# Attention kernel: the second layer's modulation accumulated in a PSUM bank of its own, PV and value transposes on the other bank, GpSimd's low weight parts in two halves

## The chip, the cores and the metric

The kernel is one program on one core of a Trainium2 chip. A core has TensorE (PE in the profile), VectorE (DVE), ScalarE (ACT), GpSimd (POOL) and SyncE (SP), which here only issues DMAs. The metric is the device time of one execution in microseconds (us), the median of several runs. Less is better.

## The reference, cut to what matters

A network of two layers works on 1024 latent tokens and 256 context tokens of width 1024. Layer 0 is grouped-query attention, layer 1 a convolution module. Each layer is wrapped in a modulation: from a condition vector `c` one linear map gives a shift, a scale and a gate.

```python
for i in range(2):
    shift, scale, gate = split(silu(c) @ ada_w[i] + ada_b[i])      # 1024 -> 3 x 1024
    h = rmsnorm(x, norm_g[i]) * (1 + scale) + shift
    if i == 0:   # 16 query heads, 4 key/value heads of 128, rotary positions
        q, k, v, z = split(h @ w_in);  kc, vc = the same columns for the context
        p = softmax([sink, q @ kc.T, q @ k.T where |i - j| <= 128])
        y = ((p @ [vc, v]) * silu(z)) @ w_out
    else:        # pointwise GLU, depthwise convolution of width 31, layer norm, gate
        y = conformer(h)
    x = x + gate * y
out = rmsnorm(x, final_g)
```

Everything is in float32. The kernel computes each large product from a high and a low part of both operands (three of the four partial products), so each weight chunk is split: the high part is a rounded copy, the low part is what the copy lost.

## The kernel before

**Stages.** First come layer 0's shift and scale, the turned and normalised tokens (tiles `hh` and `hl`, high and low), and the projections k, q, v of head group 0. Then the attention stage walks through 128 steps, one for each of 16 heads and 8 blocks of 128 queries. Between its own products TensorE computes there the projections of later heads, 12 matmuls a step (`fill`). Then follow attention's output projection, layer 1's input projection with the convolution, and the output projection.

**A step of attention.** `scores` (line 967) forms the scores of the next block in a PSUM tile `pss`; VectorE adds the mask and takes the maximum (the custom operation into `p_page`), ScalarE takes exponentials, VectorE a reciprocal (`sc`), GpSimd scales the probabilities. `transposes` (line 1001) turns the current block's probabilities on TensorE; ScalarE and VectorE evacuate them as `pthi` and `ptlo`. Once four blocks are there, `pv` (line 1022) multiplies them with the values into a PSUM tile `pso`, and VectorE evacuates it with the gate path into `oz_half`.

**Change of the key group.** After heads 3, 7 and 11 the projections k and v of the next group run whole. `vt_split` (line 550) turns a piece of v into `pso`, and ScalarE and VectorE evacuate it as `vh` and `vl`. The order on TensorE is: context piece, first half, `pv` of the old head's second half, scores of the new head, second half.

**The modulation that is left over.** `ada_rest` (line 582) is a generator that the steps advance once or twice each. It computes layer 0's gate and all of layer 1's modulation on VectorE: 16 chunks of 256 columns, 8 row blocks each. SP loads a block of 128x256 raw weights into one of two buffers (`dww_raw`, `wsum_raw`). VectorE multiplies it by the condition and adds it to the accumulator `acc_a`, 256 columns of the tile `mask_page` in SBUF. In a chunk's first block two small operations add the bias on a diagonal. After the eighth block TensorE sums over the partitions by a product with a column of ones into a tile `pso`. A gate chunk goes back into the first row of `acc_a` and from there to DRAM (`gd`); another goes into `mod1`.

**Banks.** `ps_o()` (line 128) gives one of two PSUM banks (512 columns each), in turn unless a number is asked for. `pv`, `vt_split` and `ada_rest` took turns. In the projections of group 0 the turns of x tiles ask for bank 0 or 1 by the parity of their index.

**Weight chunks.** `WStream.split` (line 221) makes a chunk's high part on ScalarE (`whi_page`) and its low part (`wlo_page`, 128x1024) on VectorE or, for all of the attention's chunks but the first four, on GpSimd. Layer 1's chunks take another branch of it, which isn't changed. `low_parts` splits the output weights on ScalarE (`lhi_half`) and GpSimd (`low_page`) and stores their low parts to DRAM (`wolA`, `wolC`).

**What sets the order.** TensorE's instructions stay in the order of the program. For the other engines and the DMA queues a planner lays out the order beforehand: it simulates the program with costs of its own and takes, of what is ready, what stands earliest or has its priority raised. On the chip every queue runs in that order. Accesses to one PSUM bank by two engines are kept apart by waits.

## Time and profile before

| what | value |
|---|---|
| runs | 1755.21, 1755.38, 1758.65 us; median 1755.38 |
| profiled execution | span of 1752.9 us; its own run time isn't listed beside the three, whose median is 2.5 us above the span |
| granted TensorE clock | 0.996 on the mean |
| TensorE busy | 1720.7 us, 98% of the span |
| VectorE, ScalarE, GpSimd busy | 1148.3, 889.4, 895.4 us |
| accumulations of `ada_rest` | first at 67.8 us, last at 824.6 us |

The span goes from the first to the last instruction. An engine's busy time is the union of its instructions' spans. All of this kernel's instructions are recorded under one line, a helper's, so the profile is read by the names of the tiles: `pss<-kh_page,qh_page` is a product of keys and queries into a tile `pss`.

### The profile page before, as it was taken

Reading aid. Unit: us, or ns where it says so; the run is one execution under the profiler, and the core shown is the slowest. Engines: PE = TensorE matmul, PEld = TensorE weight load, DVE = VectorE, ACT = ScalarE, POOL = GpSimd, SP = SyncE. Lnnn points to the kernel's source line nnn. Section 1 sums busy time; section 2 is a strip of 40 time slices with the busy share of each in tenths; the row PEclk is TensorE's granted clock in tenths of the full one; section 3 lists DMA queues with packets and bytes.
Section 4 is the critical chain, followed back from the end, with each engine's and each line's share of the span. In section 5 each row is a group of like instructions: output and inputs, shape, how many; then the busy total and the mean of one; then the engine's idle time right before and its main releaser. Section 6 shows DMA issues by size and latency. Waiting matters only on the chain.

```text
span 1752.9 us, 23877 instructions
## 1 busy us (share of the span) xinstructions
PE 1720.7 (98%) x8420; PEld 1424.8 (81%) x8420; DVE 1148.3 (66%) x2079; ACT 889.4 (51%) x1548; POOL 895.4 (51%) x705
## 2 busy tenths in 40 slices
PE   7999999999999999999999999999999999999997
PEld 4788888888888888888888888888888888788886
DVE  6755564556546563656315189999999999867823
ACT  7555553445345444545334355554665564466731
POOL 0245654566636565653101267998898888130300
PEclk9999999999999999999999999999999999999999
DMA  9334443444334542436777733011121202377971
GB/s 313 107 82 139 136 133 85 145 147 145 100 105 143 152 142 87 136 119 203 279 250 239 241 90 105 13 54 31 43 79 36 91 30 79 120 254 243 325 264 48
DMA packets 195324, 242.45 MB, mean 138 GB/s; under 512 B 11798, under 2 KB 126790, under 8 KB 195204
## 3 DMA queue, kind: packets, MB, share of 16 engines
q1 hardware_dynamic: 188516, 230.10, 40.3%
q10 hardware_dynamic: 6688, 10.83, 2.6%
q8 instruction: 66, 1.08, 0.3%
q14 instruction: 54, 0.44, 0.1%
HBM read 188.70 MB, written 41.69 MB: 131 GB/s over the span
## 4 chain that ended last, share of the span: by engine, by line
PE 86%; DMA 5%; DVE 3%; POOL 2%; ACT 2%; issue 2%; SPq 1%; ACTq 0%; POOLq 0%; DVEq 0%
PE psg L89 44%; PE pss L89 22%; PE pso L89 19%; DMA araw_page<-in_ada_w_dram 1%; POOL rope_half L89 1%; DMA low_page<-in_conv_w_out_dram 1%; DMA rope_half<-rope_half 1%; SPq L89 1%; DMA low_page<-in_attn_w_out_dram 1%; DMA wolC<-low_page 1%; DVE mask_page L89 1%; ACT p_page L89 0%; POOL wlo_page L89 0%; POOL low_page L89 0%; DMA wraw_page<-in_attn_w_in_dram 0%
## 5 line engine op out<-in xcount | busy, mean ns | idle before, releaser
L89 POOL TENSOR_TENSOR odd_half<-odd_half,prod_half 128x513 f32<-128x513 f32 (+2 forms) x252 | 312.8, 1250 | 24.2 <-ACT prod_half L89 11.0
L89 PE MATMUL psg<-hh_page,whi_page 128*128 128x512 f32 x600 | 237.6, 396 | 0.0
L89 PE MATMUL psg<-hh_page,wlo_page 128*128 128x512 f32 x600 | 236.9, 395 | 0.0
L89 PE MATMUL psg<-hl_page,whi_page 128*128 128x512 f32 x600 | 236.8, 395 | 0.0
L89 POOL TENSOR_TENSOR wlo_page<-wraw_page,whi_page 128x1024 fp32r<-128x1024 f32 x70 | 173.1, 2475 | 104.1 <-ACT whi_page L89 83.2
L89 ACT ACTIVATE prod_half<-ubuf,dww 128x513 f32<-128x513 f32 (+2 forms) x252 | 165.1, 674 | 107.3 <-POOL odd_half L89 105.1
L89 POOL TENSOR_SCALAR p_page<-p_page,sc 128x640 f32<-128x640 f32 (+1 forms) x128 | 100.8, 787 | 224.4 <-DVE sc L89 208.7
L89 PE MATMUL psg<-h2h_page,whi_page 128*128 128x512 f32 x464 | 183.9, 396 | 0.0
L89 PE MATMUL psg<-h2h_page,wlo_page 128*128 128x512 f32 x464 | 183.0, 394 | 0.0
L89 PE MATMUL psg<-h2l_page,whi_page 128*128 128x512 f32 x464 | 182.4, 393 | 0.0
L89 DVE SCALAR_TENSOR_TENSOR pss<-ubuf,dww,pss 128x512 f32<-128x512 f32 (+3 forms) x270 | 172.3, 670 | 0.1
L89 DVE SCALAR_TENSOR_TENSOR pss<-ubuf,wsum,pss 128x512 f32<-128x512 f32 (+3 forms) x270 | 171.7, 670 | 0.2
L89 DVE TENSOR_TENSOR ptlo<-pss,pthi 128x640 fp32r<-128x640 f32 (+1 forms) x144 | 103.3, 717 | 64.0 <-ACT pthi L89 62.8
L89 ACT ACTIVATE p_page<-p_page,sc 128x641 f32<-128x641 f32 (+1 forms) x128 | 102.7, 802 | 74.1 <-DVE sc L89 69.7
L89 ACT ACTIVATE pthi<-pss 128x640 fp32r<-128x640 f32 (+1 forms) x144 | 88.6, 615 | 91.7 <-PE pss L89 86.3
L89 PEld LDWEIGHTS psg<-hh_page,wlo_page 128*128 128x128 f32 x600 | 112.9, 188 | 26.3
L89 PEld LDWEIGHTS psg<-hh_page,whi_page 128*128 128x128 f32 x600 | 113.0, 188 | 20.8 <-DVE kvc_page L89 0.2
L89 PEld LDWEIGHTS psg<-hl_page,whi_page 128*128 128x128 f32 x600 | 112.9, 188 | 20.7
L89 ACT ACTIVATE whi_page<-wraw_page 128x1024 fp32r<-128x1024 f32 x88 | 92.6, 1053 | 69.0 <-PE psg L89 25.5
L89 PE MATMUL pso<-h2l_page,whi_page 128*128 128x512 f32 x304 | 119.9, 394 | 0.0
L89 PE MATMUL pso<-h2h_page,whi_page 128*128 128x512 f32 x304 | 119.8, 394 | 0.0
L89 PE MATMUL pso<-h2h_page,wlo_page 128*128 128x512 f32 x304 | 119.6, 394 | 0.0
(244 smaller groups left out, 4105.2 us busy)
## 6 DMA issues: line engine op xcount, KB each, us to landing
wraw_page<-in_conv_w_in_dram SPq DMA_DIRECT2D x48, 512.0 KB
wraw_page<-in_attn_w_in_dram SPq DMA_DIRECT2D x40, 512.0 KB
wol_page<-wolA SPq DMA_DIRECT2D x32, 512.0 KB
wo_page<-in_attn_w_out_dram SPq DMA_DIRECT2D x32, 512.0 KB
wo_page<-in_conv_w_out_dram SPq DMA_DIRECT2D x32, 512.0 KB
wol_page<-wolC SPq DMA_DIRECT2D x32, 512.0 KB
rope_half<-rope_half ACTq DMA_DIRECT2D x80, 128.0 KB
araw_page<-in_ada_w_dram SPq DMA_DIRECT2D x32, 256.0 KB
```

Of the source, the lines that this page charges most:

```text
L89: r = f(*a, **k)
```

## The change

There are three edits. The accumulator of `ada_rest` becomes columns 0 to 255 of PSUM bank 1, which it holds for its whole life; TensorE's sum goes into columns 256 to 511 of the same bank, and before that sum ScalarE copies the accumulator to its old place in `mask_page`, with raised priority. `vt_split` and `pv` always ask for bank 0. And where GpSimd makes a chunk's low part in the unraised branch of `split`, it does so in two operations of half the chunk each.

```diff
@@ WStream.split
-                split_lo(self.lo_eng(i), l, r, h)
+                if self.lo_eng(i) is G:
+                    for a in range(0, KT, KT // 2):
+                        split_lo(G, *(t[:, a:a + KT // 2] for t in (l, r, h)))
+                else:
+                    split_lo(self.lo_eng(i), l, r, h)
@@ vt_split
-        tp = ps_o()
+        tp = ps_o(0)
@@ ada_rest
         load(0)
+        bank = ps_o(1)
+        acc, o = bank[:, 0:256], bank[:, 256:512]
         for i, (l, c0, kt) in enumerate(todo):
...
             if kt == 0:
-                after(V.tensor_scalar(out=acc_a, in0=raw, scalar1=cs[:, kt:kt + 1], scalar2=None, op0=ALU.mult))
+                after(V.tensor_scalar(out=acc, in0=raw, scalar1=cs[:, kt:kt + 1], scalar2=None, op0=ALU.mult))
                 for b in range(2):
...
-                    stt(acc_a[:, bs], ident, abt[:, col:col + 1], acc_a[:, bs], ALU.mult, ALU.add)
+                    stt(acc[:, bs], ident, abt[:, col:col + 1], acc[:, bs], ALU.mult, ALU.add)
             else:
-                after(stt(acc_a, raw, cs[:, kt:kt + 1], acc_a, ALU.mult, ALU.add))
+                after(stt(acc, raw, cs[:, kt:kt + 1], acc, ALU.mult, ALU.add))
             yield
             if kt < KT - 1:
                 continue
+            with tc.high_priority():
+                act(acc_a, acc, AF.Copy)
             yield
-            o = ps_o()
             if c0 >= 2048:
-                PE.matmul(o[0:1, 0:256], ones[:, 0:1], acc_a, start=True, stop=True)
-                V.tensor_copy(acc_a[0:1], o[0:1, 0:256])
+                PE.matmul(o[0:1], ones[:, 0:1], acc_a, start=True, stop=True)
+                V.tensor_copy(acc_a[0:1], o[0:1])
                 SY.dma_start(out=gd[l][:, c0 - 2048:c0 - 1792], in_=acc_a[0:1])
             else:
                 for b in range(2):
                     PE.matmul(o[:, b:b + 1], acc_a[:, b * P:b * P + P], ones[:, 0:1], start=True, stop=True)
                 V.tensor_copy(mod1[:, c0 // P:c0 // P + 2], o[:, 0:2])
@@ pv
-        o = ps_o()
+        o = ps_o(0)
```

## The prediction

> **What bounds the kernel now.** I read the busy shares first, then busy time by stage, then TensorE's own waits inside the stage that the change touches. From the page's first part and from the busy time of each engine in five stretches (columns: stretch, length, then busy us and instruction count of PE, PEld, DVE, ACT, POOL; granted clock; DMA share; GB/s):

> ```profile
> span 1752.9 us, 23877 instructions
> PE 1720.7 (98%) x8420; PEld 1424.8 (81%) x8420; DVE 1148.3 (66%) x2079; ACT 889.4 (51%) x1548; POOL 895.4 (51%) x705
> ...
> 0.00:97.00 97.00, 83.66 (x402) 57.59 (x403) 62.57 (x114) 60.42 (x92) 13.58 (x17) 0.96 0.60 190
> 97.00:850.00 753.00, 745.04 (x4107) 642.27 (x4106) 424.05 (x832) 368.79 (x776) 412.08 (x340) 1.00 0.44 136
> 850.00:1050.00 200.00, 200.00 (x914) 163.27 (x913) 75.31 (x154) 74.08 (x115) 43.91 (x40) 1.00 0.62 208
> 1050.00:1500.00 450.00, 448.51 (x1937) 363.97 (x1936) 430.46 (x682) 256.71 (x360) 383.24 (x281) 1.00 0.19 57
> 1500.00:1753.00 253.00, 243.53 (x1067) 197.69 (x1065) 155.95 (x300) 129.43 (x206) 42.58 (x28) 0.99 0.62 215
> ```

> TensorE is the bound everywhere. The attention stage, where almost all of the change takes effect, runs from about 97 to 850 us; TensorE is busy for 745.04 of its 753 us. So 8 us is all that a perfect change of that stage could win, 0.45% of the time. The clock is at 1.00 there and the change adds no matrix work, so what counts is only which of those idle times go and which come. VectorE and GpSimd are 56% and 55% busy in that stage: their busy time alone buys nothing. TensorE's waits in it (columns: who waited for whom; us in total, times, longest):

> ```profile
> PE pss L89 <- DVE ptlo L89: 3.6, 2, 3.2
> PE pss L89 <- DVE sc L89: 1.3, 3, 0.9
> PE pss L89 <- POOL hl_page L89: 1.2, 1, 1.2
> PE psg L89 <- DVE rope_half L89: 1.0, 1, 1.0
> PE pss L89 <- POOL p_page L89: 0.5, 1, 0.5
> ```

> These are 7.6 of the 8 us, in eight waits. No wait on the tile pso, the two banks that the change rearranges, is among them.

> **Step 1: the accumulator moves to PSUM.** The 112 multiply-adds now read two tensors from SBUF (the raw weights and the accumulator in mask_page). The convolution stage does the same operation with its accumulator in PSUM, and is the nearest row for the price after. From the groups with shapes kept apart (count | busy us, mean ns):

> ```profile
> L89 DVE SCALAR_TENSOR_TENSOR mask_page<-wsum_raw,cs,mask_page 128x256 f32<-128x256 f32 x64 | 51.3, 801 | 0.1
> L89 DVE SCALAR_TENSOR_TENSOR mask_page<-dww_raw,cs,mask_page 128x256 f32<-128x256 f32 x48 | 38.4, 800 | 3.0 <-DMA dww_raw<-in_ada_w_dram 2.9
> L89 DVE SCALAR_TENSOR_TENSOR pss<-ubuf,dww,pss 128x264 f32<-128x264 f32 x30 | 14.0, 490 | 0.0
> L89 DVE SCALAR_TENSOR_TENSOR pss<-ubuf,dww,pss 128x248 f32<-128x248 f32 x30 | 13.3, 468 | 0.0
> ```

> Halfway between 490 and 468 is 479 ns for 256 columns. The operation gets 0.32 us shorter on the mean, 112 x 0.32 = 36 us of VectorE (estimate). Why it is 801 now shows in the stretch around 546 us (start us, us, engine, operation, [idle before it and what ended that]):

> ```profile
> 544.88 1.28 POOL L89 TENSOR_TENSOR low_page<-low_page,lhi_half 128x512 f32<-128x512 f32 x1
> 545.18 1.26 DVE L89 SCALAR_TENSOR_TENSOR mask_page<-wsum_raw,cs,mask_page 128x256 f32<-128x256 f32 x1
> 546.36 0.87 DVE L89 CUSTOM_DVE_ANT_0 p_page<-pss,mask_page,nsink 128x640 f32<-128x640 f32 x1
> ...
> 547.30 0.44 PE L89 MATMUL pss<-kh_page,qh_page 128*128 128x384 f32 x1 [0.19 <-DVE sc L89]
> ```

> The multiply-add starts while GpSimd runs a two-input subtraction, ends 0.28 us after it (546.16), and takes 1.26 us; the softmax's mask-and-maximum waits behind it on VectorE, and TensorE waits for that. All three waits on "DVE sc" have such a stretched operation just ahead of that maximum. With 0.48 us in place of 1.26, 0.78 us come back, more than the 0.19 lost here; I take the whole 1.3 us. The 48 other small operations on the accumulator are not counted; shorter ones could only help the same three places. Each raw buffer is free for SP's next load up to 0.78 us earlier; the number of DMAs is unchanged.

> VectorE also stops waiting where an accumulation could not begin before a gate row had left mask_page:

> ```profile
> DVE mask_page L89 <- DMA gd<-mask_page: 5.8, 4, 2.0
> ```

> None of TensorE's eight waits lies behind those four, so I count nothing for 5.8 us of VectorE.

> **Step 2: 16 copies on ScalarE, and the low parts in halves.** The rows for both prices:

> ```profile
> L89 ACT ACTIVATE pthi<-pss 128x256 fp32r<-128x256 f32 x32 | 12.1, 378 | 15.2 <-PE pss L89 11.5 <-DVE ptlo L89 3.2
> L89 POOL TENSOR_TENSOR wlo_page<-wraw_page,whi_page 128x1024 fp32r<-128x1024 f32 x70 | 173.1, 2475 | 104.1 <-ACT whi_page L89 83.2 <-PE pss L89 13.9 <-PE psg L89 3.5
> L89 POOL TENSOR_TENSOR low_page<-low_page,lhi_half 128x512 f32<-128x512 f32 x64 | 83.7, 1307 | 0.0
> ```

> A copy of 128x256 out of PSUM is 0.38 us: 16 are 6.0 us on an engine that is 49% busy in this stage. Behind a copy stand the exponentials and the evacuations of transposed probabilities. A copy waits for the eighth multiply-add; in the stretch above VectorE follows that with 0.87 us of maximum, for which ScalarE's next exponential must wait anyway, and 0.38 fits in. I take 0, with 6.0 (each copy wholly on the path) as the other end. The product with the column of ones is issued a generator step later, so TensorE should not meet the copy.

> Each of the 36 GpSimd splits of this stage becomes two of 128x512, 2 x 1.31 against 2.48: 0.14 us more, 5 us in all on an engine that is 55% busy; TensorE waits for none of them. What it buys is an opening between the halves. Around 720 us:

> ```profile
> 719.17 2.44 POOL L89 TENSOR_TENSOR wlo_page<-wraw_page,whi_page 128x1024 fp32r<-128x1024 f32 x1
> 719.25 0.16 DVE L89 RECIPROCAL sc<-sc 128x1 f32<-128x1 f32 x1 [0.99 <-ACT p_page L89]
> ...
> 721.60 1.63 POOL L89 TENSOR_SCALAR p_page<-p_page,sc 128x640 f32<-128x640 f32 x2
> ...
> 722.62 0.55 PE L89 MATMUL pss<-ident,p_page 128*128 128x128 f32 x3 [0.53 <-POOL p_page L89]
> ```

> The probabilities could be scaled from 719.41 (719.25 + 0.16), but GpSimd is inside the low part until 721.61. In halves the scaling could start at 719.17 + 1.31 = 720.48, 1.1 us earlier. The planner puts it there if it ranks the scaling, which stands earlier in the program, ahead of the second half. I take the whole 0.5 us; the other end is 0.

> **Step 3: one bank for PV and the value transposes.** They took turns on two banks; now all use bank 0. Between PV groups four query blocks pass, so only neighbours in program order can meet. There are two kinds. First, head 0's first value transposes, issued right behind the turn of an x tile that also sits in bank 0:

> ```profile
> 82.86 0.60 PE L89 MATMUL pso<-ident,x_page 128*128 128x128 f32 x4
> 83.30 0.60 PE L89 MATMUL pso<-ident,vf_half 128*128 128x128 f32 x4
> 83.50 0.78 ACT L89 ACTIVATE hh_page<-pso,mod 128x512 fp32r<-128x512 f32 x1 [2.61 <-PE pso L89]
> ...
> 84.31 0.81 DVE L89 TENSOR_SCALAR hf_page<-pso,mod 128x512 f32<-128x512 f32 x1 [1.85 <-ACT hh_page L89]
> ...
> 86.50 0.44 PE L89 MATMUL pso<-ident,x_page 128*128 128x128 f32 x2 [0.52 <-DVE vl_page L89]
> ```

> At present they start at 83.30 in bank 1. In bank 0 they must wait for both readers of the x tile, to 84.31 + 0.81 = 85.12, and TensorE, in program order, stands for 1.82 us. In exchange the next x tile, in bank 1, no longer waits 0.52 for the value transposes. Net +1.3 us (ends: 1.3 and 1.8).

> Second, at the three changes of key group the last value transposes follow PV after six score products:

> ```profile
> 295.60 0.28 PE L89 MATMUL pso<-pthi,vl_page 128*128 128x256 f32 x1
> ...
> 295.91 0.69 DVE L89 SCALAR_TENSOR_TENSOR oz_half<-pso,zs_page 128x512 f32<-128x512 f32 x1 [6.33 <-PE pso L89]
> ...
> 296.41 0.60 PE L89 MATMUL pso<-ident,vf_half 128*128 128x128 f32 x4
> ```

> PV's evacuation ends at 296.60, so the transposes move from 296.41 to 296.60 or a little later: 0.2 us, three times, +0.6 us (ends: 0, and 3 x 0.69 if VectorE is busy when PV ends; it had idled 6.33 us).

> The accumulator's first operations need bank 1, which the last x tile holds until about 97 us. Two generator steps that could start earlier now fall after that: at most 4 x 0.49 = 2 us of VectorE work. I take 0, since none of the waits above stands there.

> **The sum.** -1.3 (sc) - 0.5 (p_page) + 1.3 (first transposes) + 0.6 (three group changes) + 0 = +0.1 us, against a span of 1752.9 us. The runs' median of 1755.38 lies 2.5 us above the span; I carry that over: 1755.5 us. About 0.2% (3.5 us) is what a measurement of this kernel can tell from no change, so this is no change.

> **The rivals.** *More waits fall.* The largest wait is not mine yet. At 588 us:

> ```profile
> 588.64 1.15 ACT L89 ACTIVATE lhi_half<-low_page 128x512 fp32r<-128x512 f32 x2 [5.95 <-DMA low_page<-in_conv_w_out_dram]
> ...
> 591.29 0.44 PE L89 MATMUL pss<-kh_page,qh_page 128*128 128x384 f32 x1 [3.19 <-DVE ptlo L89]
> ```

> ScalarE stood 5.95 us for a landing, with the evacuation of transposed probabilities behind it. If earlier releases on SP bring that load forward, or the planner orders ScalarE otherwise, the 3.6 us of ptlo go, and with VectorE freer the 1.0 us of rope_half: -1.3 - 0.5 - 3.6 - 1.0 + 1.9 = -4.5, 1750.9 us, faster. For it: all these are eight chance meetings, and a new order rarely repeats one. Against: that landing is no work of VectorE.

> *Another landing in the way* (the other side). The same mechanism, at a new place: ScalarE at the head of its queue waits for a low-part load, the probabilities queue behind it, and TensorE pays 3.2 us each time. The planner lays out a new order for ScalarE, with 16 more instructions in it, and does not know when a DMA lands. One such hit in addition to the present one makes 1755.5 + 3.2 = 1758.7; from the second it is decidedly slower: 1755.5 + 6.4 = 1761.9 us. Against it: one hit in 64 low-part splits so far.

> *The copies hurt.* If ScalarE reaches each of them too early, all 16 lie on the path: 1755.5 + 6.0 = 1761.5 us. For it: they are raised in priority, and an engine takes its queue in order. Against: the 0.87 us of cover in step 2.

> *The change doesn't do what it says.* VectorE may be slower with PSUM than the convolution's rows tell. The far row is a scale-and-shift, 128x512:

> ```profile
> L89 DVE TENSOR_SCALAR hf_page<-pso,mod 128x512 f32<-128x512 f32 x22 | 17.4, 805 | 19.1 <-PE pso L89 11.3 <-ACT hh_page L89 7.3 <-ACT p_page L89 0.5
> L89 DVE TENSOR_SCALAR xn_page<-x_page,r 128x512 f32<-128x512 f32 x16 | 6.9, 481 | 0.2
> ```

> Out of PSUM 805, out of SBUF 481: 0.32 us more, just what the change should save. Then the 1.3 us of sc stay: 1756.8 us. I give it little, because the same operation with its accumulator in PSUM is the 479 ns of step 1.

> [...]

> **How the numbers follow.** Chances: my sum 0.45; the copies at a part of their price or the accumulator no faster, both within 0.2%, 0.05; more waits fall 0.26; another landing 0.16; the copies at full price 0.08. So faster 0.26, same 0.50, slower 0.24. The likeliest case has its own range from the ends of its terms: 1754.9 (group changes free) to 1758.0 (0.5 more at the first transposes, 1.5 more at the group changes, no gain of 0.5 from the halves). The range over all cases runs from 1749.5, the faster rival without the 1.3 us at the first transposes, to 1762, the two slower ones.

> **What would show it.** The multiply-adds into pso at about 0.48 us, with none over 1 us; no "PE pss <- DVE sc" wait behind them; a scaling of probabilities between two halves of a low part; a new wait of about 1.8 us of TensorE near 83 us, before value transposes; three of about 0.2 us at the group changes. TensorE's idle time between 97 and 850 us should stay within 5 to 9 us. I would be wrong if that total left this band: look first at ScalarE's waits for low_page loads, then at its waits for VectorE before the copies.

## The result and the profile after

The changed kernel takes 1759.97 us (median of 19 runs, 1755.55 to 1763.05), against 1755.68 us for the kernel before in the same series (median of 19 runs). The ratio is 1.0023 with a 95% interval of 1.0017 to 1.0029: some 4.0 us slower. The profiled execution of the changed kernel has a span of 1755.7 us and a time of 1757.52 us, so it is one of the quicker ones. Against the profile of before the span is only 2.8 us longer.

From the page's first part, and then from the busy time by stage (columns as in the prediction), of the changed kernel:

```profile
span 1755.7 us, 23938 instructions
PE 1721.7 (98%) x8420; PEld 1425.1 (81%) x8420; DVE 1104.0 (63%) x2079; ACT 896.1 (51%) x1564; POOL 897.0 (51%) x741
```

```profile
0.00:97.00 97.00, 83.74 (x400) 58.01 (x401) 62.05 (x109) 59.84 (x90) 13.50 (x17) 0.96 0.58 187
97.00:850.00 753.00, 743.08 (x4094) 640.73 (x4093) 379.12 (x834) 374.75 (x793) 412.79 (x375) 1.00 0.44 135
```

VectorE is 44 us less busy, ScalarE 6.7 us more, and TensorE nevertheless idles 9.9 us between 97 and 850 us instead of 8.0. TensorE's waits in this stretch, in the changed kernel (us in total, times, longest):

```profile
PE pso L89 <- ACT mask_page L89: 3.3, 1, 3.3
PE pss L89 <- DVE ptlo L89: 2.7, 1, 2.7
PE psg L89 <- DVE rope_half L89: 1.5, 1, 1.5
PE pss L89 <- POOL hl_page L89: 1.2, 1, 1.2
PE pss L89 <- POOL p_page L89: 0.4, 1, 0.4
PE pso L89 <- DVE oz_half L89: 0.3, 2, 0.2
```

The waits on "DVE sc" are gone. A new one stands in first place: once in the whole run, for 3.3 us, TensorE waits for ScalarE's copy of the accumulator. It is the copy of the sixteenth and last chunk, at 826 us. The stretch around it in the changed kernel (start us, us, engine, operation, [idle before it and what ended that]):

```profile
822.71 0.71 PE L89 MATMUL pss<-ident,p_page 128*128 128x128 f32 x5
822.80 1.06 ACT L89 ACTIVATE ozh_page<-ozf_page 128x1024 fp32r<-128x1024 f32 x1 [0.79 <-DMA ozf_page<-ozd]
823.10 0.48 DVE L89 SCALAR_TENSOR_TENSOR pso<-wsum_raw,cs,pso 128x256 f32<-128x256 f32 x1
...
823.86 0.82 ACT L89 ACTIVATE p_page<-p_page,sc 128x641 f32<-128x641 f32 x1
...
824.67 0.58 ACT L89 ACTIVATE zs_page<-psg 128x512 f32<-128x512 f32 x1
...
825.30 1.06 ACT L89 ACTIVATE woh_page<-wo_page 128x1024 fp32r<-128x1024 f32 x1
826.27 0.36 ACT L89 ACTIVATE mask_page<-pso 128x256 f32<-128x256 f32 x1
...
826.68 0.59 PE L89 MATMUL pso<-mask_page,ones 128*1 128x256 f32 x2 [3.26 <-ACT mask_page L89]
```

The accumulator is complete at 823.58. From there ScalarE is never idle, but it works through an exponential, a gate evacuation and the rounding of an output weight first: the copy comes 2.69 us after the data, although its priority is raised. TensorE, in program order, has the product with the column of ones next; it reached it at 823.42 and stands. The kernel before had no room at this place either:

```profile
824.57 0.48 DVE L89 SCALAR_TENSOR_TENSOR mask_page<-wsum_raw,cs,mask_page 128x256 f32<-128x256 f32 x1
...
825.10 0.09 PEld L89 LDWEIGHTS pso<-mask_page,ones 128*1 128x1 f32 x2 [0.36 <-DVE mask_page L89]
825.10 0.59 PE L89 MATMUL pso<-mask_page,ones 128*1 128x256 f32 x2
```

There the accumulation ended at 825.05, and the sum's weight load, which had waited 0.36 us for it, began at 825.10. The wait is one of a weight load (PEld), so it does not stand among the waits of the matmuls that the prediction lists. The other fifteen accumulations of that trace ended 2.1 to 10.5 us before their sums. In the changed kernel the other fifteen copies have room. The fifteenth, for instance:

```profile
779.92 0.48 DVE L89 SCALAR_TENSOR_TENSOR pso<-wsum_raw,cs,pso 128x256 f32<-128x256 f32 x1
780.44 0.39 ACT L89 ACTIVATE mask_page<-pso 128x256 f32<-128x256 f32 x1 [1.20 <-DVE pso L89]
...
782.54 0.59 PE L89 MATMUL pso<-mask_page,ones 128*1 128x256 f32 x2
```

The copy follows the data at once and is done 1.7 us before TensorE needs it. In the code the last two chunks are alike: the generator is advanced twice in the attention step of the eighth accumulation, so the accumulation and the copy fall into one step and the sum into the next (in the other fourteen the copy comes a step after the accumulation). What differs in the last chunk is the other work. In the last head ScalarE also rounds the operands of attention's output projection (`ozh_page` and `woh_page`, 1.06 us each), and VectorE splits them (`ozl_page`, 1.23 us from 820.41, directly ahead of the maximum and of the evacuation that the accumulation follows). That this work makes the accumulation and the copy late is read from the order in the trace; no run leaves it out.

Pairing the 8420 matmuls of both traces in their order shows where TensorE falls behind. The left column is the time in the trace of before:

| where | after less before |
|---|---|
| start to 82 us | -0.7 us |
| first value transposes, 82 to 97 us | +1.2 |
| three changes of the key group | +0.43, +0.37, +0.38 |
| the three former waits on sc, 353, 374, 547 us | -1.2, -0.4, -0.5 |
| 226, 395, 588 us (softmax and ptlo waits) | -0.4, -0.7, -0.5 |
| 277 us (rope_half, now 1.5 in place of 1.0) | +0.5 |
| last sum and the matmuls behind it, 823 to 829 us | +4.7 |
| all the rest | -0.4 |
| whole span | +2.8 |

The first row isn't the change: in the eight kernels below it lies anywhere from -1.3 to +1.3 us. Without it the rows give +3.5 us, near the 4.0 of the medians. Until 820 us the changed kernel was 1.5 us ahead, 0.7 of them from the first row; one place turned that round.

Of the 4.7 us there, 3.3 are the wait; the rest is a clock that was granted at 0.50 for 3.41 us behind it, from 827.31 us on. From busy time by stretch, changed kernel:

```profile
823.30:826.70 3.40, 0.14 (x3) 0.02 (x2) 2.26 (x4) 3.34 (x8) 0.80 (x1) 1.00 0.99 365
826.70:830.20 3.50, 3.50 (x12) 2.77 (x13) 2.04 (x4) 1.79 (x4) 0.21 (x1) 0.59 1.02 393
830.20:834.00 3.80, 3.80 (x22) 3.31 (x21) 0.16 (x1) 2.57 (x4) 0.80 (x1) 0.93 1.04 393
```

At a granted clock of 0.59 TensorE gets 12 matmuls done in 3.5 us; the kernel before did 20 in the 3.5 us from 826.5 at a clock of 1.00.

### The profile page after: what moved, and what is told of

Its sections match the earlier page's. It is cut to its first block, busy times and chain, and to the rows that moved or that the text cites. A ratio compares the mean times of both kernels' runs of the same rounds, so it can differ in the third digit from the quotient of the medians.

```text
span 1755.7 us, 23938 instructions
## 1 busy us (share of the span) xinstructions
PE 1721.7 (98%) x8420; PEld 1425.1 (81%) x8420; DVE 1104.0 (63%) x2079; ACT 896.1 (51%) x1564; POOL 897.0 (51%) x741
## 4 chain that ended last, share of the span: by engine, by line
PE 88%; DMA 6%; POOL 2%; DVE 2%; ACT 1%; issue 1%; SPq 1%; ACTq 0%; POOLq 0%; DVEq 0%
PE psg L89 46%; PE pss L89 23%; PE pso L89 19%; DMA low_page<-in_conv_w_out_dram 1%; DMA araw_page<-in_ada_w_dram 1%; DMA rope_half<-rope_half 1%; POOL rope_half L89 1%; SPq L89 1%; DMA x_page<-in_x_dram 0%; DMA wolC<-low_page 0%; POOL wlo_page L89 0%; DMA wraw_page<-in_attn_w_in_dram 0%; DMA ozf_page<-ozd 0%; POOL p_page L89 0%; POOL low_page L89 0%
## 5 line engine op out<-in xcount | busy, mean ns | idle before, releaser
L89 POOL TENSOR_TENSOR odd_half<-odd_half,prod_half 128x513 f32<-128x513 f32 (+2 forms) x252 | 313.2, 1251 | 24.1 <-ACT prod_half L89 10.7
L89 PE MATMUL psg<-hh_page,whi_page 128*128 128x512 f32 x600 | 237.3, 395 | 0.0
L89 PE MATMUL psg<-hh_page,wlo_page 128*128 128x512 f32 x600 | 236.8, 395 | 0.0
L89 PE MATMUL psg<-hl_page,whi_page 128*128 128x512 f32 x600 | 236.5, 394 | 0.0
L89 POOL TENSOR_TENSOR wlo_page<-wraw_page,whi_page 128x512 fp32r<-128x512 f32 (+1 forms) x106 | 178.8, 1703 | 103.6 <-ACT whi_page L89 81.7
L89 ACT ACTIVATE prod_half<-ubuf,dww 128x513 f32<-128x513 f32 (+2 forms) x252 | 165.3, 675 | 110.3 <-POOL odd_half L89 108.0
L89 POOL TENSOR_SCALAR p_page<-p_page,sc 128x640 f32<-128x640 f32 (+1 forms) x128 | 99.6, 778 | 228.0 <-DVE sc L89 218.6
L89 PE MATMUL psg<-h2h_page,whi_page 128*128 128x512 f32 x464 | 183.7, 396 | 0.0
L89 PE MATMUL psg<-h2h_page,wlo_page 128*128 128x512 f32 x464 | 182.8, 394 | 0.0
L89 PE MATMUL psg<-h2l_page,whi_page 128*128 128x512 f32 x464 | 182.2, 393 | 0.0
L89 DVE SCALAR_TENSOR_TENSOR pss<-ubuf,dww,pss 128x512 f32<-128x512 f32 (+3 forms) x270 | 172.5, 671 | 0.1
L89 DVE SCALAR_TENSOR_TENSOR pss<-ubuf,wsum,pss 128x512 f32<-128x512 f32 (+3 forms) x270 | 171.8, 671 | 0.2
L89 DVE TENSOR_TENSOR ptlo<-pss,pthi 128x640 fp32r<-128x640 f32 (+1 forms) x144 | 103.4, 718 | 74.9 <-ACT pthi L89 73.6
L89 ACT ACTIVATE pthi<-pss 128x640 fp32r<-128x640 f32 (+1 forms) x144 | 88.9, 617 | 104.6 <-PE pss L89 99.3
L89 ACT ACTIVATE p_page<-p_page,sc 128x641 f32<-128x641 f32 (+1 forms) x128 | 102.6, 802 | 67.5 <-DVE sc L89 63.8
L89 PEld LDWEIGHTS psg<-hh_page,wlo_page 128*128 128x128 f32 x600 | 112.7, 188 | 26.4
L89 PEld LDWEIGHTS psg<-hl_page,whi_page 128*128 128x128 f32 x600 | 112.8, 188 | 20.9
L89 PEld LDWEIGHTS psg<-hh_page,whi_page 128*128 128x128 f32 x600 | 112.9, 188 | 20.6
L89 ACT ACTIVATE whi_page<-wraw_page 128x1024 fp32r<-128x1024 f32 x88 | 92.7, 1053 | 66.4 <-PE psg L89 26.0
L89 PE MATMUL pso<-h2l_page,whi_page 128*128 128x512 f32 x304 | 119.7, 394 | 0.0
L89 PE MATMUL pso<-h2h_page,whi_page 128*128 128x512 f32 x304 | 119.7, 394 | 0.0
L89 PE MATMUL pso<-h2h_page,wlo_page 128*128 128x512 f32 x304 | 119.5, 393 | 0.0
```

Of the source, the lines that this page charges most:

```text
L89: r = f(*a, **k)
```

## The experiments

The leading theory: the loss is one place, the last sum, and without it the change comes out where the prediction put it. The rivals: the shared bank 0 costs more than forecast; the copies cost something everywhere; the longer GpSimd work in halves hurts. All ratios are to the kernel before, run on the same chip in the same series, with 95% intervals; the medians of before were 1756.18 us (first four) and 1757.03 us (last four).

**The last sum a step later.** The changed kernel, with one edit in `ada_rest`:

```diff
             yield
+            if i == len(todo) - 1:
+                yield
             if c0 >= 2048:
```

> The changed kernel with one more generator step between the last chunk's copy and its sum on TensorE. Theory A (one place): nearly all of the loss is TensorE's 3.3 us wait for ScalarE's last copy at 823 us, and the half clock behind it (about 8 matmuls at 0.43 instead of 0.23 us, 1.5 us). Both go: 4.6 us less than the changed kernel, ratio to the kernel before 0.9985 to 1.0005, TensorE idle between 97 and 850 us about 6 us. Theory B (spread): the copies, the shared bank and the new order cost a little everywhere, and the wait at 823 only collects a delay that would be paid elsewhere: ratio stays at 1.0015 or more, with a new wait of 2 us or more later.

Measured: 1755.98 us, 0.9995 [0.9986, 1.0005]. From its timeline:

```profile
824.10 0.48 DVE L89 SCALAR_TENSOR_TENSOR pso<-wsum_raw,cs,pso 128x256 f32<-128x256 f32 x1
...
826.24 0.36 ACT L89 ACTIVATE mask_page<-pso 128x256 f32<-128x256 f32 x1
...
828.63 0.59 PE L89 MATMUL pso<-mask_page,ones 128*1 128x256 f32 x2
```

The copy runs when it ran in the changed kernel (826.24 us, there 826.27), at the same place in ScalarE's order, and ends 2.0 us before the sum. Here only the sum has moved, and TensorE does not meet the copy. Against the changed kernel's 1.0023 this is 0.28% less, 4.9 us, and the row of the table says 4.7. One place out of sixteen carried the whole loss, within these intervals. The result is also a measurement of the prediction's sum without that place: no difference, where +0.1 us was forecast. The interval is 3.3 us wide, and the terms of the sum came out otherwise than forecast (below), so that the two agree is in part luck.

**The last copy on VectorE.** The changed kernel, with the last chunk's copy as `V.tensor_copy`:

```diff
-                act(acc_a, acc, AF.Copy)
+                if i == len(todo) - 1:
+                    V.tensor_copy(acc_a, acc)
+                else:
+                    act(acc_a, acc, AF.Copy)
```

> The changed kernel with the last chunk's copy on VectorE, the other 15 on ScalarE. If ScalarE's queue is the cause (the copy stood behind an exponential, a gate evacuation and a weight copy), VectorE does it right behind the last accumulation: TensorE waits 1 us or less there, no half clock, ratio 0.999 to 1.001. If the last accumulation itself is too late for the sum, TensorE still waits 2 us or more and the ratio stays above 1.0015.

Measured: 1758.57 us, 1.0011 [1.0002, 1.0020], between the two cases of the expectation. TensorE's wait at the place, and then VectorE's order there, in this kernel:

```profile
PE pso L89 <- DVE mask_page L89: 1.7, 1, 1.7
```

```profile
827.11 0.48 DVE L89 SCALAR_TENSOR_TENSOR pso<-wsum_raw,cs,pso 128x256 f32<-128x256 f32 x1
827.50 1.22 DVE L89 TENSOR_TENSOR ozl_page<-ozf_page,ozh_page 128x1024 fp32r<-128x1024 f32 x1
828.64 0.42 DVE L89 COPY mask_page<-pso 128x256 f32<-128x256 f32 x1
```

The wait halves. VectorE does not do the copy right behind the accumulation, either: it splits an operand of the output projection first. The accumulation is complete at 827.59, 0.17 us after TensorE came to the sum, and the copy starts 1.05 us later. So 1.05 of the 1.69 us are VectorE's queue, as 2.69 of the 3.26 us in the changed kernel are ScalarE's. With no queue at all the copy and the late accumulation would leave some 0.6 us (an estimate from these rows).

**The banks alone.** The kernel before, with bank 0 for `vt_split` and `pv` and bank 1 for `ada_rest`'s sum; the accumulator stays in SBUF, and there are no copies and no halves:

```diff
@@ vt_split
-        tp = ps_o()
+        tp = ps_o(0)
@@ ada_rest
-            o = ps_o()
+            o = ps_o(1)
@@ pv
-        o = ps_o()
+        o = ps_o(0)
```

> The kernel before, with PV and value transposes on bank 0 and the modulation's sums on bank 1, accumulator still in SBUF, low parts whole. The prediction's step 3 alone: 1.3 us at the first value transposes and three times 0.2 us at the group changes, +1.9 us, ratio 1.0005 to 1.0015. If the sharing costs nothing on balance: 1.000. If it is the main loss: 1.002 or more. The waits behind stretched accumulations (1.3 us) stay.

Measured: 1758.77 us, 1.0015 [1.0006, 1.0024]. TensorE's waits hold these lines, first those before 97 us, then those between 97 and 850 us:

```profile
PE pso L89 <- DVE hf_page L89: 1.7, 1, 1.7
```

```profile
PE pss L89 <- DVE ptlo L89: 3.0, 1, 3.0
...
PE pss L89 <- DVE sc L89: 0.6, 2, 0.5
...
PE pso L89 <- DVE oz_half L89: 0.3, 2, 0.2
```

Matmul by matmul it loses 1.2 us between 82 and 97 us and 0.35 us at each group change, 2.2 us, as in the changed kernel: this is the price of sharing the bank, 0.13% of the 0.15% measured. The sc waits fell from 1.3 to 0.6 us without any change of the accumulator, so a part of that gain came with the new order alone.

**The changed kernel without the halves.**

```diff
-                if self.lo_eng(i) is G:
-                    for a in range(0, KT, KT // 2):
-                        split_lo(G, *(t[:, a:a + KT // 2] for t in (l, r, h)))
-                else:
-                    split_lo(self.lo_eng(i), l, r, h)
+                split_lo(self.lo_eng(i), l, r, h)
```

> The changed kernel with GpSimd's low parts whole again. In the changed kernel's trace the wait for scaled probabilities near 720 us is still there (0.4 against 0.5 us), so the halves buy about nothing: theory A gives the changed kernel's ratio, 1.0018 to 1.0030, with the 3.3 us wait in place. If the halves had been what cost (5 us more of GpSimd), this is at 1.000; if they were what helped, above 1.003.

Measured: 1758.64 us, 1.0015 [1.0006, 1.0024]. Its waits between 97 and 850 us:

```profile
PE pss L89 <- DVE ptlo L89: 3.4, 1, 3.4
PE pso L89 <- ACT mask_page L89: 2.3, 1, 2.3
```

The ratio lies below the 1.0018 to 1.0030 that were expected, but its interval overlaps that of the changed kernel. The wait for the last copy is there without halves, too, 2.3 us long, so the halves do not cause it.

**The halves alone**, on the kernel before (the three lines above, put in).

> The kernel before with GpSimd's low parts in halves and nothing else. Three traces with PSUM accumulation show no gain from the halves (0.4 us waited for scaled probabilities with them, 0.5 without in the kernel before). If so: 0.9995 to 1.0005. The prediction's step 2 had 0.5 us, 0.9997; shorter blocks of VectorE's accumulations could add to that: 0.999.

Measured: 1755.97 us, 0.9995 [0.9986, 1.0004]. The wait that the halves should have removed (TensorE's waits, 97 to 850 us), and the accumulations that still stand in SBUF (groups with shapes kept apart, same stretch):

```profile
PE pss L89 <- POOL p_page L89: 1.0, 1, 1.0
```

```profile
L89 DVE SCALAR_TENSOR_TENSOR mask_page<-wsum_raw,cs,mask_page 128x256 f32<-128x256 f32 x63 | 43.0, 682 | 0.4 <-DMA wsum_raw<-in_ada_w_dram 0.3
```

The wait on p_page grew from 0.5 to 1.0 us: around 719 us both halves ran one behind the other, and the scaling still came after them. In the changed kernel it never stands between two halves: in all 36 chunks the second half starts 1.24 to 1.29 us after the first, with nothing between. What did get shorter with the halves is VectorE's multiply-adds: 682 ns on the mean in place of 806 in this stretch. The sc waits are 0.4 us here in place of 1.3; how much of that comes from the shorter operations and how much from the new order was not separated.

**The first value transposes back in bank 1**, on top of the later sum:

```diff
+    vbank = [1]
...
-        tp = ps_o(0)
+        tp = ps_o(vbank.pop() if vbank else 0)
```

> late_sum with the first value transposes on bank 1, which the accumulator does not hold yet. The wait of 1.7 us at 83 us should go and the old one of 0.5 us at the next x tile come back: 1.2 us less than late_sum, ratio 0.998 to 0.9995. If TensorE only reaches the next wait of the prologue earlier: as late_sum, 0.9995.

Measured: 1755.34 us, 0.9994 [0.9986, 1.0003]. The 1.7 us wait at 83 us is gone and the loss between 82 and 97 us is 0.0 in place of 1.2. But 1.2 us can't be read from the medians here: the interval is 3 us wide, and in the profiled execution another wait grew to 2.0 us, again with a reduced clock behind it (below). The gain at this place is shown by the trace, not by the times.

**A later step for one low-part load.** The largest wait that is left when the last sum is moved is the one at 588 us. The prediction read it as ScalarE standing for a load of low_page. The kernel before, with one more step between load and split of that item:

```diff
             SY.dma_start(out=raw, in_=src)
             yield "open"
+            if n == 23:
+                yield "open"
```

> The kernel before, with the 24th output weight's split one step later behind its load. If the landing at 588 us is what holds ScalarE, TensorE's 3.2 us wait there goes: 1.8 us less at a granted clock of 1.00, and in executions where the half clock follows the stall another 1.6 us: ratio 0.997 to 0.9985. If the probabilities wait for something else: a wait of 2 us or more stays at 588 us, ratio 1.000.

Measured: 1758.19 us, 1.0003 [0.9993, 1.0014]. A wait of 2.6 us stayed, and ScalarE's order shows that the edit did not reach the split:

```profile
587.28 1.15 ACT L89 ACTIVATE lhi_half<-low_page 128x512 fp32r<-128x512 f32 x2 [5.52 <-DMA low_page<-in_conv_w_out_dram]
588.33 0.68 ACT L89 ACTIVATE pthi<-pss 128x640 fp32r<-128x640 f32 x1
```

The split stands where it stood, directly ahead of the transposed probabilities, and waits 5.52 us in place of 5.95. The extra step did not move it in the order that the planner laid out. What did move is the order elsewhere: the sc waits rose from 1.3 to 3.5 us. Whether the wait at 588 us falls when that split really comes later was not shown.

**Later sum, bank 1 and later step together.**

> late_sum_bank1 and late_landing together. If the costs are separate places, they add: 0.5 to 1.5 us (late_sum) + 1.2 us (bank 1) + 3 to 4.5 us (landing) less than the kernel before, ratio 0.9957 to 0.9975. If the planner's new order opens another wait of that size: 0.998 or more.

Measured: 1755.30 us, 0.9990 [0.9982, 0.9999]. That is the second case of the expectation, but not for its reason. It is the only one of the eight whose interval lies wholly below 1, and only just; it can't be told from the kernel with the later sum and bank 1 (0.9994). Its waits are led by the same one at 588 us, 3.1 us long, so no new wait opened, and the gain expected from that part never came. It is faster than the changed kernel; a gain of 0.1% over the kernel before is at the limit of what these runs show.

## Why the prediction was wrong in its sum and right in most of its steps

The forecast of 1755.5 us and "no change" missed by 4.5 us against the median of 1759.97 us, although the time lies within the range. It lies above the 1758.0 us to which the likeliest case was to reach, and no rival describes what happened; that the range held it is luck, for it was that wide because of rivals that did not come. The term that failed is the copies' 0, by 4.7 us. The halves' 0.5 us did not come either, and the group changes cost twice their term.

**Step 1 held.** The multiply-adds were to take 0.48 us, none over 1 us. They take this (changed kernel, groups with shapes kept apart, 97 to 850 us):

```profile
L89 DVE SCALAR_TENSOR_TENSOR pso<-wsum_raw,cs,pso 128x256 f32<-128x256 f32 x64 | 30.8, 481 | 0.1
...
L89 DVE SCALAR_TENSOR_TENSOR pso<-dww_raw,cs,pso 128x256 f32<-128x256 f32 x48 | 23.1, 481 | 0.4 <-DMA dww_raw<-in_ada_w_dram 0.3
```

The views by tile, first of the changed kernel, then of the kernel before, show the spread (shortest/median/longest ns, first and last start):

```profile
L89 DVE SCALAR_TENSOR_TENSOR pso<-wsum_raw,cs,pso x64: 477/480/490, 102.2 to 823.1; 128x256 f32<-128x256 f32 x64
```

```profile
L89 DVE SCALAR_TENSOR_TENSOR mask_page<-wsum_raw,cs,mask_page x64: 468/484/2203, 68.8 to 824.6; 128x256 f32<-128x256 f32 x64
```

481 ns against 479 forecast, and none over 490, where before one took 2203. The rival in which PSUM makes VectorE no faster is out: half of the operations of before, with the accumulator in SBUF, took 484 ns or less, and half of those with it in PSUM 480 or less; by the median PSUM cost nothing here, and the mean fell from 801 to 481 ns. One of the small operations did get longer at the median: a chunk's first multiplication, which only writes the accumulator, took 353 ns before and 477 ns after. Its mean between 97 and 850 us still fell, from 605 to 476 ns, because none is stretched any more (before, up to 1344 ns). The 1.3 us of sc waits were taken whole; the three places gave 2.1 us. The rest of the surplus, 1.6 us at 226, 395 and 588 us, less 0.5 us at rope_half, is the prediction's "more waits fall" in small. How much of it is the shorter operation and how much the new order stays open: with the accumulator in SBUF other orders brought sc to 0.6 (banks alone), 0.4 (halves alone) and 3.5 us (later step for a load). With it in PSUM, no sc wait in any of these traces has an accumulation directly ahead of the maximum.

**Step 2 failed.** "I take 0" for the sixteen copies was right for fifteen. The reason given for the sum, "issued a generator step later, so TensorE should not meet the copy", counts steps of the program and not time. It was never set against the time that lies between an accumulation and its sum: in the trace of before that is 2.1 us or more at fifteen places and 0.06 us at the last, so a copy of 0.38 us could not fit in there even with ScalarE free. ScalarE then was not free. I worked out what a copy does to the work behind it on ScalarE, and not what the work ahead of it does to the copy. The rival "the copies hurt" looked the same way: ScalarE too early, 0.38 us sixteen times, 6.0 in all. It was ScalarE too late, once, for 3.3 us. The -0.5 us for the halves failed as well: the wait was 0.4 us in place of 0.5, and the planner never used the opening.

**Step 3 held in kind, and one of its two terms in size.** Net +1.3 us at the first value transposes: +1.2 measured. For the wait itself 1.82 us were forecast from the end of the second reader of the x tile. From the timeline of the changed kernel:

```profile
83.60 0.81 DVE L89 TENSOR_SCALAR hf_page<-pso,mod 128x512 f32<-128x512 f32 x1 [1.90 <-ACT hh_page L89]
84.46 0.66 PE L89 MATMUL pso<-ident,vf_half 128*128 128x128 f32 x4 [1.72 <-DVE hf_page L89]
```

The three changes of the key group were put at 0.2 us each and cost 0.4. The first of them in the changed kernel:

```profile
297.28 0.63 PE L89 MATMUL pso<-ident,vf_half 128*128 128x128 f32 x4 [0.16 <-DVE oz_half L89]
```

These transposes stood at 296.41. They are 0.87 us later; the kernel was 0.49 us behind when it came there, so 0.4 us is new, of which the profile shows 0.16 as a wait. Forecast were 0.6 us for the three, and 1.2 us came.

**The sum, redone.** -2.1 (sc) + 1.2 (first transposes) + 1.2 (group changes) - 1.1 (other waits) + 0 (halves) = -0.8 us without the last copy, and +3.9 us with its 4.7. The first figure agrees with the kernel with the later sum (0.9995, about -0.9 us), the second with the measured 4.0 us. The prediction's own sign that it was wrong, TensorE idle for more than 9 us between 97 and 850 us, came in at 9.9, and the second place named to look at was near it: not the copy's wait for VectorE, but TensorE's wait for the copy.

## What to carry to other kernels

A step that is added between a producer and an engine that runs in program order has to be costed at every place where it occurs, and first at the one with the least distance between them: here fifteen copies cost nothing and the sixteenth 4.7 us. That distance can be read from the trace of before, as the time from the producer's end to the consumer's start. Raised priority did not bring the short copy past what the planner had put ahead of it in an engine's queue, on ScalarE or on VectorE; moving the consumer one step later took the wait away. And 44 us less of VectorE's busy time were worth 1 to 3 us, because little of it was ever waited for.

## What the hardware showed beyond that

```profile
586.61:590.02 3.41, 1.49 (x10) 1.02 (x8) 0.00 (x0) 1.38 (x3) 0.00 (x0) 1.00 0.72 240
590.02:593.44 3.42, 2.15 (x12) 1.94 (x13) 2.71 (x7) 3.28 (x7) 1.64 (x2) 1.00 0.17 48
```

```profile
275.98:279.40 3.42, 1.45 (x13) 1.22 (x12) 1.01 (x2) 0.43 (x1) 2.38 (x2) 1.00 0.44 106
279.40:282.81 3.41, 3.41 (x18) 3.41 (x18) 1.40 (x3) 2.33 (x4) 2.39 (x2) 0.50 0.42 125
```

The long stall fell across a boundary, with 1.9 us of idle time in one window and 1.3 us in the next. The short one lay in one window whole, and the next window ran at a clock of 0.50.

Over the ten traces, between 97 and 850 us, stalls of 2.0, 2.3, 2.8, 3.0, 3.1, 3.1, 3.3, 3.4 and 3.8 us were followed by a reduced clock, and stalls of 1.7, 2.4, 2.6, 2.7 and 3.2 us were not. Length alone does not part the two groups, but idle time within one window does: in this stage each of the nine windows in which TensorE stood for 1.97 us or more was followed by a reduced clock, and no window in which it stood for 1.92 us or less was. The two sides are 0.05 us apart, with one window each there, so the limit is known only roughly. Before 97 us that does not hold; there the clock also dropped behind windows with less than 1 us of idle time (0.77 us in the changed kernel's window that ends at 18.35 us). In the changed kernel the drop of one window cost 1.4 us, the 4.7 us at that place less the wait of 3.3. In eight of the nine drops between 97 and 850 us the clock was back after one window, 3.41 us. In the kernel with all three edits together the stall reached 0.63 us into the next window, and the clock stayed down for two windows, 6.83 us.

From the 1.4 us of the changed kernel the estimate is that a small stall that comes or goes with a reordering, or that falls otherwise across the windows, can be worth some 1.4 us more in one execution than in the next. The clock goes with a part of the scatter between runs here and not with all of it: over the 35 runs of the kernel before in the second series, times from 1753.32 to 1761.27 us correlate with the mean granted clock (0.993 to 0.998) at -0.55.
